# Output products of two attention layers as planned pieces, and bias tables by two rounded-format products

## The chip, the cores and the metric

The kernel runs on one core of one Trainium2 chip. The metric is the device time of one execution in microseconds (us). The engines are PE (TensorE, matrix products; PEld is its weight load), DVE (VectorE), ACT (ScalarE), POOL (GpSimd) and SP (SyncE, which here only issues transfers).

## The reference

All inputs are float32, one sequence of 256 tokens, model width 1024. Three blocks follow each other and share the residual `h`:

- Layer A: `h += dsa_mixer(rms_norm(h)) `, attention with 16 heads of 64. An indexer picks the best 64 keys per query; the logits get a bias `rel_bias[bucket(key - query)]` per head, then softmax, the product with `v`, and `out @ a_w_o` (1024 x 1024). An MLP with a squared ReLU follows (1024 to 4096 to 1024).
- Layer B: `h += mla_mixer(...)`, attention with 16 heads of 96 on low-rank keys and queries, and `out @ b_w_o` (1024 x 1024). The same kind of MLP follows.
- A hybrid layer: an mLSTM, three groups of dilated window attention with 8 heads each, whose logits get a bias from `rel_bias_2`, gates, an output product, and a gated MLP.

The changed parts are the two products `out @ a_w_o` and `out @ b_w_o` and the four bias tables: one of 16 heads for layer A, three of 8 heads for the window groups. A table holds, for each head, the bias at each of 512 relative positions. It is made as a product of the 32 bucket values (plus one row for positions that are masked) with a constant 0/1 matrix `c_oh` of 33 x 512.

## The kernel before

The 256 tokens are two tiles of 128, called t (0 and 1). Each large product is computed in a rounded float32 format (fp32r): an operand is split into a high part and a low rest (`split`, `wsplit`: the high part by a copy on ACT, the rest by a subtraction on DVE), and three products are summed: high x high, high x low, low x high (`mm_tok`, L275, L276, L278).

A weight piece is 512 contraction rows by 512 columns. It comes by one transfer of 1 MB on SP's queue (L247) into one of 3 `raw` buffers, and is split into one of 4 pairs of `hi`/`lo` buffers (L252 on ACT, L255 on DVE).

An output product of an attention layer is four PSUM banks, (t, ci) with ci the half of the 1024 columns. Each bank sums over two groups g of four contraction tiles, that is heads 0 to 7 and heads 8 to 15. A bank takes 24 products of 512 columns, 12 for each g. `out_proj` (L300) loads and splits the four weight pieces and then calls `mm_tok` for the four banks, t outermost. `add_res` (L315) adds a bank to the residual. The banks are the two buffers of the tag `acc`.

The order of instructions on each engine is made by a scheduler of the language from the program's order: an instruction that comes earlier in the program has the higher rank, and where it isn't ready, a later one may go first. Inside the attention layers the program's order is itself written out by hand. `weave` (L525) walks a plan: a name runs an item, `*n` runs n rounds of the attention pipeline, `**` all that are left. A round runs f1 of a step (logits, maximum, exponential), f2 of the step before (transposes of the probabilities) and f3 of the one before that (product with `v`). A step handles two heads of one token tile. In PLAN_A `s`, `k`, `q`, `t` are scores, top-k, query projection and its transposes. In PLAN_B `k`, `q`, `2`, `3` with a group number are key and query projections of four heads, their scaling, and their transposes into `KTb`/`QT`; `o` with t and a half is the transposes of the attention's output. `out_proj` stands behind the whole plan in both layers, so its instructions have the lowest rank there. Its weight splits are held behind chosen instructions (`behind`): in layer A behind the two top-k masks (`picked`), in layer B behind the last copies of the groups 2 and 3 (`made`).

A bias table is made by `bias_rows` (L438): the constant matrix comes by SP's queue into a buffer of the tag `pT` (2 buffers, also used by the attention for its transposed probabilities), one plain float32 product writes PSUM, ACT copies it, and ACT's queue stores it to memory. It is called once in layer A, before the attention, and three times in the first MLP. `rb` (L450) holds the bucket values, 16 columns for layer A and 24 for the window groups.

Of the kernel before, what the change touches and what calls it, by code (L numbers as in the profile page):

```python
# [10 lines left out]
F32 = mybir.dt.float32  # L11
# [6 lines left out]
P = 128  # L18
# [6 lines left out]
NACC, NTR, NLG, NPO = 2, 2, 3, 1  # L25


PLAN_A = "s0 k0 q0 q1 t00 t01 s1 * t10 k1 *4 t11 **"
PLAN_B = "k0 q0 k2 20 q1 k1 30 21 *2 q2 31 * 22 k3 q3 *2 32 *4 23 *2 o00 33 *5 o10 *2 o01 o11"
PLAN_C = "ck mg ms cq q0 mw k0 mn v0 v1 ml B0 *2 q1 *3 B1 *3 o0 k1 *3 k2 * v2 * q2 B2 o1 *2 a0 *2 a1 * b1 * p0 p1 *4 b0 *3"  # L30


# [57 lines left out]
def block_kernel(ctx: ExitStack, tc: tile.TileContext, a, out: bass.AP):  # L90
# [24 lines left out]
    def tpt(s):  # L115
        return sp.tile([P, 512], F32, tag="pT", name=nm(s), bufs=NPT)
# [171 lines left out]
    def dense_by_tile(jobs, holds=(None, None)):  # L288
# [5 lines left out]
        for t in range(2):  # L294
            for pr, (x, KT, _, _, n, _, evac) in zip(parts, jobs):
                ps = acc("acc")
                mm_tok(ps[:, :n], x, t, pr, KT)
                evac(t, ps[:, :n])

    def out_proj(x, w, scale=None, holds=(None, None)):  # L300
        dense_by_tile([(x, 8, w, 512 * ci, 512, None, lambda t, ps, ci=ci: add_res(t, ci, ps, scale))
                       for ci in range(2)], holds)
# [78 lines left out]
    def mlp(i):  # L381
# [46 lines left out]
        for c in range(2, 8):  # L428
            step(c - 2)
            up(c)  # L430
            if i == 0 and 3 <= c <= 5:
                bias_rows(c - 2, 33, 8, 8 * c - 8, vec_b[c - 3])
        last([6, 7], r2)

    def len_u(u):
        return u[0][0].shape[1]

    def bias_rows(which, K, M, c0, vec):  # L438

        oh = tpt("oh")  # L440
        nc.sync.dma_start(oh[:33, :], a["c_oh"][:, which, :])
        ps = trp("bt")
        PE.matmul(ps[:M, :], rb[:K, c0:c0 + M], oh[:K, :], start=True, stop=True)
        sb = tj("bts")
        A.activation(sb[:M, :], ps[:M, :], AF.Copy)
        nc.scalar.dma_start(vec, sb[:M, :])

    vec_a = dr.tile([16, 512], F32, name="vec_a")
    vec_b = [dr.tile([8, 512], F32, name=f"vec_b{g}") for g in range(3)]
    rb = cp.tile([33, 40], F32, name="rb")  # L450
    gcols = {}

    def ldk(dst, src):
        tc.keep_in_program_order(nc.sync.dma_start(dst, src))

    def load_consts():
        V.memset(rb[32:33, :], 1.0)
        chmask = t2("chmask")[:, :256]
        ldk(chmask, a["c_sq"][:, 512:768])
        ldk(rb[:32, 0:16], a["rel_bias"])  # L460
        ldk(rb[:32, 16:40], a["rel_bias_2"])
        for nm_, src in (("kv", a["kv_norm"]), ("q", a["b_attn_norm"][0])):
            gcols[nm_] = cp.tile([P, 8], F32, name="gc" + nm_)
            ldk(gcols[nm_], src.rearrange("(k p) -> p k", p=P))
        return chmask
# [108 lines left out]
    def layer_a():  # L574
# [24 lines left out]
                mm_tok(ps[:, :356], x, t, wkv[ci], 8)  # L599
                A.activation(kvi[t][:, ci * 356:(ci + 1) * 356], ps[:, :356], AF.Copy, scale=rs[t])  # L600
        chmask = load_consts()
        bias_rows(0, 32, 16, 0, vec_a)

        KT = t4("KT").rearrange("p (a n) -> p a n", a=4)
        qiT, w8 = [], []
# [71 lines left out]
        def q_T(t, ci):  # L677
            tp = transposes(qn[t, ci], 4)
            A.activation(qT[t][:, ci * 512:(ci + 1) * 512], tp, AF.Copy)
# [22 lines left out]
        for i in range(2):  # L702
            items["s%d" % i] = lambda i=i: scores(i)
            items["k%d" % i] = lambda i=i: topk(i)
            items["q%d" % i] = lambda i=i: dense(x, 8, w, [(512 * i, 512)], lambda t, _, ps: ev_q(t, i, ps), gain=gcol)
            for ci in range(2):
                items["t%d%d" % (i, ci)] = lambda i=i, ci=ci: q_T(i, ci)
        weave(PLAN_A, items, steps)
        out_proj(oT, a["a_w_o"][0], holds=picked)

    identb = cp.tile([P, P], BF, name="identb")
    V.tensor_copy(identb, ident)
# [1 line left out]
    def layer_b():  # L714
# [185 lines left out]
        for gi in range(4):  # L900
            for c, f in zip("kq23", proj(gi)):
                items[c + str(gi)] = f
        for c in '00 01 10 11 20 21 30 31'.split():
            steps += attend(int(c[0]), int(c[1]))
        for t in range(2):
            for i in range(2):
                items["o%d%d" % (t, i)] = lambda t=t, i=i: o_T(t, i)
        weave(PLAN_B, items, steps)
        out_proj(oT, a["b_w_o"][0], holds=(made[2], made[3]))

    def block2():
        w = a["w_in_2"][0]
# [413 lines left out]
```

## Time and profile before

| | |
|---|---|
| three runs, us | 1152.83, 1156.35, 1156.69; median 1156.35 |
| profiled execution | 1153.44 us, its span 1151.3 us |
| PE | 1124.7 us busy (98%), 6912 matrix products and transposes |
| PEld | 992.4 us (86%) |
| DVE, ACT, POOL | 678.6 us (59%), 614.1 us (53%), 68.4 us (6%) |
| granted clock of PE, mean | 0.998 |
| moved | 191.92 MB, 167 GB/s |

The span is counted from the profile's start; all stretches below are in us from there. A busy share is the time in which an engine had an instruction under way. Layer A's attention is worked on from about 56 to 114 us, the first MLP from 122 to 308, layer B's attention from about 340 to 398. In the rows, "idle before" stands in square brackets with what ended it.

### The profile page before, as it was taken

The numbers are of one execution on the slowest core, as the hardware profiler recorded it, in microseconds if no ns is written. First come the engines' busy times: TensorE is split into PE (matmuls) and PEld (weight loads), VectorE is DVE, ScalarE is ACT, GpSimd is POOL, SyncE is SP. The second block draws the span as 40 slices with busy tenths as digits, with TensorE's granted clock in tenths as the row PEclk, the third lists the DMA queues.
The fourth block names the chain that finished last, engine by engine and source line by source line (L and its number), as shares of the span: only waits on it lengthen the run. The fifth ranks groups of instructions, "written<-read, shape, count | busy, mean of one in ns | idle before, by whom it ended". The sixth has DMA issues, their size and how long they took to land.

```text
span 1151.3 us, 17271 instructions
## 1 busy us (share of the span) xinstructions
PE 1124.7 (98%) x6912; PEld 992.4 (86%) x6912; DVE 678.6 (59%) x1224; ACT 614.1 (53%) x1070; POOL 68.4 (6%) x80
## 2 busy tenths in 40 slices
PE   7989999999998999999999999999999999999997
PEld 6767898889897879989989999888888878999996
DVE  6794754445688574554366976645475566544544
ACT  7654555445487555554446664555554435433443
POOL 1210000000043000000000000010000030000000
PEclk9999999999999999999999999999999999999999
DMA  9540646554462346565538444744544535546641
GB/s 282 199 147 23 216 151 222 182 184 132 132 212 75 104 147 214 170 219 184 171 107 281 147 147 148 240 143 147 183 147 153 183 122 178 206 154 213 202 141 61
DMA packets 105383, 191.92 MB, mean 167 GB/s; under 512 B 6616, under 2 KB 22960, under 8 KB 105304
## 3 DMA queue, kind: packets, MB, share of 16 engines
q1 hardware_dynamic: 104056, 187.16, 48.6%
q0 software_dynamic: 1040, 3.54, 1.0%
q8 instruction: 54, 0.88, 0.3%
q14 instruction: 25, 0.20, 0.1%
q10 hardware_dynamic: 208, 0.13, 0.0%
HBM read 189.68 MB, written 1.13 MB: 166 GB/s over the span
## 4 chain that ended last, share of the span: by engine, by line
PE 92%; DVE 4%; ACT 1%; issue 1%; DMA 0%; POOL 0%; SPq 0%; POOLq 0%; DVEq 0%; ACTq 0%
PE acc L275 10%; PE acc L276 10%; PE acc L278 9%; PE dn L361 7%; PE dn L362 7%; PE dn L364 7%; PE up L310 5%; PE up L313 5%; PE up L311 5%; PE tr L165 3%; PE po L509 2%; PE qk L310 2%; PE qk L311 2%; PE lg L485 2%; PE qk L313 2%; PE fp L310 1%
## 5 line engine op out<-in xcount | busy, mean ns | idle before, releaser
L255 DVE TENSOR_TENSOR wlo<-raw,whi 128x1024 fp32r<-128x1024 f32 (+3 forms) x340 | 385.5, 1177 | 211.3 <-ACT whi L252 211.1
L252 ACT ACTIVATE whi<-raw 128x1024 fp32r<-128x1024 f32 (+3 forms) x340 | 322.9, 1007 | 212.3 <-PE dn L364 86.7
L310 PE MATMUL up<-mxh,whi 128*128 128x256 f32 x448 | 110.9, 281 | 0.0
L311 PE MATMUL up<-mxl,whi 128*128 128x256 f32 x448 | 110.7, 280 | 0.0
L361 PE MATMUL dn<-whi,uh 128*128 128x512 f32 x256 | 100.7, 395 | 0.0
L362 PE MATMUL dn<-wlo,uh 128*128 128x512 f32 x256 | 100.6, 394 | 0.0
L158 POOL TENSOR_TENSOR rr<-rv,mhalf 128x1 f32<-128x1 f32 (+2 forms) x42 | 39.8, 950 | 821.5 <-DVE rv L156 806.2
L310 PEld LDWEIGHTS up<-mxh,whi 128*128 128x128 f32 x448 | 84.3, 188 | 0.7
L311 PEld LDWEIGHTS up<-mxl,whi 128*128 128x128 f32 x448 | 84.2, 188 | 0.7
L275 PE MATMUL acc<-whi,cxh 128*128 128x512 f32 (+1 forms) x192 | 74.5, 389 | 0.0
L276 PE MATMUL acc<-wlo,cxh 128*128 128x512 f32 (+1 forms) x192 | 72.3, 378 | 0.0
L313 PE MATMUL up<-mxh,wlo 128*128 128x256 f32 x448 | 71.0, 280 | 0.0
L364 PE MATMUL dn<-whi,ul 128*128 128x512 f32 x256 | 69.5, 394 | 0.0
L313 PEld LDWEIGHTS up<-mxh,wlo 128*128 128x128 f32 x448 | 60.3, 188 | 0.0
L361 PEld LDWEIGHTS dn<-whi,uh 128*128 128x128 f32 x256 | 48.1, 188 | 13.2 <-ACT whi L252 2.6
L364 PEld LDWEIGHTS dn<-whi,ul 128*128 128x128 f32 x256 | 48.1, 188 | 11.2
L362 PEld LDWEIGHTS dn<-wlo,uh 128*128 128x128 f32 x256 | 48.1, 188 | 10.6
L278 PE MATMUL acc<-whi,cxl 128*128 128x512 f32 (+1 forms) x192 | 50.6, 382 | 0.0
L169 DVE TENSOR_TENSOR ul<-sq,uh 128x512 fp32r<-128x512 f32 x28 | 19.4, 692 | 51.8 <-ACT uh L169 51.5
L310 PE MATMUL qk<-cxh,whi 128*128 128x256 f32 x192 | 49.1, 287 | 0.0
L311 PE MATMUL qk<-cxl,whi 128*128 128x256 f32 x192 | 48.2, 282 | 0.0
L493 ACT ACTIVATE lg<-lg,nx 128x128 f32<-128x128 f32 (+1 forms) x80 | 35.4, 446 | 16.3 <-DVE nx L553 16.3
(414 smaller groups left out, 2410.2 us busy)
## 6 DMA issues: line engine op xcount, KB each, us to landing
raw<-in_w_in SPq DMA_DIRECT2D x38, 1024.0 KB, 5.2
raw<-in_mlp_w_up SPq DMA_DIRECT2D x32, 1024.0 KB, 5.3
raw<-in_mlp_w_down SPq DMA_DIRECT2D x32, 1024.0 KB, 5.1
raw<-in_w_gate SPq DMA_DIRECT2D x10, 1024.0 KB, 5.5
raw<-in_w_up SPq DMA_DIRECT2D x10, 1024.0 KB, 5.1
raw<-in_w_down SPq DMA_DIRECT2D x10, 1024.0 KB, 5.0
raw<-in_w_in SPq DMA_DIRECT2D x6, 688.0 KB
raw<-in_a_w_in SPq DMA_DIRECT2D x4, 1024.0 KB
```

The costliest lines, as they stand in the source:

```text
L158: G.tensor_tensor(r[:, :n], v[:, :n], mhalf[:, :n], op=OP.pow)
L252: A.activation(hi[:, c], raw[:, c], AF.Copy)
L255: V.tensor_tensor(lo[:, c], raw[:, c], hi[:, c].bitcast(F32), op=OP.subtract)
L275: PE.matmul(o, s0, wh[:, k, :], start=(g + k == 0), stop=False)
L276: PE.matmul(o, s0, wl[:, k, :], start=False, stop=False)
L278: PE.matmul(o, xs(xl, g + k, t), wh[:, k, :], start=False, stop=(g + k == KT - 1))
L310: PE.matmul(o, s0, xh[(g + k) // 4][:, (g + k) % 4, :], start=(g + k == 0), stop=False)
L311: PE.matmul(o, s0, xl[(g + k) // 4][:, (g + k) % 4, :], start=False, stop=False)
L313: PE.matmul(o, wl[:, k, col:col + P], xh[(g + k) // 4][:, (g + k) % 4, :], start=False, stop=(g + k == KT - 1))
L361: PE.matmul(ps, s0, wh[:, k, :], start=(c == 0 and k == 0), stop=False)
L362: PE.matmul(ps, s0, wl[:, k, :], start=False, stop=False)
L364: PE.matmul(ps, xs(u[1], k, t), wh[:, k, :], start=False, stop=(c == nc_ - 1 and k == kt - 1))
```

## The change

Three things are changed.

1. `out_proj` is no longer called for the layers A and B. `out_parts` adds items to the plan: `w0` and `w1` load and split the weight pieces of one half of the columns each, `m` with t, ci and g runs the 12 products of one bank and one g. A bank is taken at g = 0 and added to the residual after g = 1. The plans place these items among the last attention rounds. The holds of the splits stay the same.
2. In layer B the order of the attention's groups and tiles is changed (group 3's first tile comes before group 2's second), `23` comes one round earlier, `33` two, `o00` and `o10` two and four.
3. The bias tables are made by two fp32r products, of the high part and of the rest of `rb`. The two parts are tiles of 33 x 128, zeroed at the start by DVE and filled by four small copies on ACT and four subtractions on DVE. The constant matrix is converted to fp32r on its way in, and this transfer is issued by POOL. All 128 PSUM rows are written; the rows of table g begin at 32 g.

```diff
-PLAN_A = "s0 k0 q0 q1 t00 t01 s1 * t10 k1 *4 t11 **"
-PLAN_B = "k0 q0 k2 20 q1 k1 30 21 *2 q2 31 * 22 k3 q3 *2 32 *4 23 *2 o00 33 *5 o10 *2 o01 o11"
+PLAN_A = "s0 k0 q0 q1 t00 t01 s1 * t10 k1 *4 t11 w0 w1 *6 m000 * m001 * m010 * m011 * m100 * m110 ** m101 m111"
+PLAN_B = "k0 q0 k2 20 q1 k1 30 21 *2 q2 31 * 22 k3 q3 *2 32 *3 23 * o00 33 w0 w1 *2 o10 *3 o01 m000 * m001 * m010 * m011 * m100 m110 o11 m101 m111"
...
+    def out_parts(items, x, w, holds):
+        parts, banks = {}, {}
+        def load(ci):
+            with behind(holds(ci)):
+                parts[ci] = wparts(w, 8, 512 * ci, 512)
+        def run(t, ci, gi):
+            if gi == 0:
+                banks[t, ci] = acc("acc")
+            g, kk, (wh, wl) = parts[ci][gi]
+            ps = banks[t, ci]
+            for k in range(kk):
+                s0 = xs(x[0], g + k, t)
+                PE.matmul(ps, s0, wh[:, k, :], start=(g + k == 0), stop=False)
+                PE.matmul(ps, s0, wl[:, k, :], start=False, stop=False)
+            for k in range(kk):
+                PE.matmul(ps, xs(x[1], g + k, t), wh[:, k, :], start=False, stop=(g + k == 7))
+            if gi == 1:
+                add_res(t, ci, ps)
+        for ci in range(2):
+            items["w%d" % ci] = lambda ci=ci: load(ci)
+            for t in range(2):
+                for gi in range(2):
+                    items["m%d%d%d" % (t, ci, gi)] = lambda t=t, ci=ci, gi=gi: run(t, ci, gi)
...
-                bias_rows(c - 2, 33, 8, 8 * c - 8, vec_b[c - 3])
+                bias_rows(c - 2, 8, vec_b[c - 3])
...
-    def bias_rows(which, K, M, c0, vec):
-        oh = tpt("oh")
-        nc.sync.dma_start(oh[:33, :], a["c_oh"][:, which, :])
+    def bias_rows(which, M, vec):
+        oh = sp.tile([P, 512], F32R, tag="pT", name=nm("oh"), bufs=NPT)
+        G.dma_start(oh[:33, :], a["c_oh"][:, which, :])
         ps = trp("bt")
-        PE.matmul(ps[:M, :], rb[:K, c0:c0 + M], oh[:K, :], start=True, stop=True)
+        for i, r in enumerate(rbs):
+            PE.matmul(ps, r[:33, :], oh[:33, :], start=i == 0, stop=i == 1)
         sb = tj("bts")
-        A.activation(sb[:M, :], ps[:M, :], AF.Copy)
-        nc.scalar.dma_start(vec, sb[:M, :])
+        m = slice(32 * which, 32 * which + M)
+        A.activation(sb[m, :], ps[m, :], AF.Copy)
+        nc.scalar.dma_start(vec, sb[m, :])
...
+    rbs = [cp.tile([33, 128], F32R, name="rb" + e) for e in "hl"]
+    for r in rbs:
+        V.tensor_scalar(r, ident[:33, :], 0.0, None, op0=OP.mult)
...
-        V.memset(rb[32:33, :], 1.0)
+        V.memset(rb[32:33, 0:16], 0.0)
+        V.memset(rb[32:33, 16:40], 1.0)
...
-        bias_rows(0, 32, 16, 0, vec_a)
+        for g, (c0, n) in enumerate(((0, 16), (16, 8), (24, 8), (32, 8))):
+            A.activation(rbs[0][:33, 32 * g:32 * g + n], rb[:33, c0:c0 + n], AF.Copy)
+            V.tensor_tensor(rbs[1][:33, 32 * g:32 * g + n], rb[:33, c0:c0 + n], rbs[0][:33, 32 * g:32 * g + n].bitcast(F32), op=OP.subtract)
+        bias_rows(0, 16, vec_a)
...
+        out_parts(items, oT, a["a_w_o"][0], lambda ci: picked[ci])
         weave(PLAN_A, items, steps)
-        out_proj(oT, a["a_w_o"][0], holds=picked)
...
-        for c in '00 01 10 11 20 21 30 31'.split():
+        for c in '00 01 10 11 20 30 21 31'.split():
...
+        out_parts(items, oT, a["b_w_o"][0], lambda ci: made[2 + ci])
         weave(PLAN_B, items, steps)
-        out_proj(oT, a["b_w_o"][0], holds=(made[2], made[3]))
```

## Rows read from the trace of the kernel before

**Rows 1.** The page's busy times: us, share of the span, instructions.

```profile
PE 1124.7 (98%) x6912; PEld 992.4 (86%) x6912; DVE 678.6 (59%) x1224; ACT 614.1 (53%) x1070; POOL 68.4 (6%) x80
```

**Rows 2.** Busy time by stretch: length, then busy us (instructions) by engine, PE clock.

```profile
core 0: us, PE busy (x) PEld busy (x) DVE busy (x) ACT busy (x) POOL busy (x), PEclk, DMA share, GB/s
...
58.00:75.00 17.00, 13.39 (x76) 9.12 (x75) 16.72 (x68) 11.64 (x42) 3.42 (x3) 1.00 0.43 155
75.00:100.00 25.00, 24.93 (x137) 18.67 (x135) 18.21 (x55) 11.69 (x40) 0.00 (x0) 1.00 0.25 85
...
398.00:417.00 19.00, 18.58 (x84) 14.60 (x84) 10.55 (x16) 7.91 (x14) 0.57 (x1) 1.00 0.26 88
```

**Rows 3.** Bias product: group of its line, then PE's timeline around the first MLP's first.

```profile
L443 PE MATMUL bt<-oh,rb 33*8 33x512 f32 (+1 forms) x8 | 4.1, 591 | 0.0
...
191.72 1.02 PE L443 MATMUL bt<-oh,rb 33*8 33x512 f32 x2
192.67 0.50 PE L361 MATMUL dn<-whi,uh 128*128 128x512 f32 x1
```

**Rows 4.** The chain that ended last: one run of eight output products, 104 to 114.

```profile
109.91 1.86 PE acc L278 x8
```

**Rows 5.** PE's timeline, end of layer A: start, us, instruction, idle before.

```profile
102.47 0.66 PE L165 MATMUL tr<-ident,o 128*128 128x128 f32 x4 [1.27 <-DVE ss L177]
...
114.28 0.66 PE L165 MATMUL tr<-ident,o 128*128 128x128 f32 x4 [0.79 <-DVE o L697]
...
115.62 0.50 PE L275 MATMUL acc<-whi,aoh 128*128 128x512 f32 x1 [0.25 <-ACT aoh L169]
...
122.17 0.47 PE L275 MATMUL acc<-whi,mxh 128*128 128x512 f32 x1 [0.31 <-DVE h L318]
```

**Rows 6.** PE's timeline, layer B's attention: its four waits from 360 to 398.

```profile
365.77 0.44 PE L165 MATMUL tr<-ident,p 128*128 128x128 f32 x2 [0.82 <-DVE QT L850]
...
368.03 0.94 PE L509 MATMUL po<-kvb,pT 128*128 128x64 f32 x4 [0.71 <-DVE pT L502]
...
373.68 0.77 PE L165 MATMUL tr<-ident,p 128*128 128x128 f32 x2 [1.19 <-ACT p L493]
...
391.21 0.77 PE L165 MATMUL tr<-ident,p 128*128 128x128 f32 x2 [0.49 <-ACT p L493]
```

**Rows 7.** Busy time by stretch around those waits, columns as in rows 2.

```profile
368.00:370.00 2.00, 1.97 (x9) 1.93 (x10) 2.00 (x4) 1.39 (x6) 0.00 (x0) 0.56 0.01 4
370.00:372.00 2.00, 2.00 (x10) 1.68 (x8) 2.00 (x3) 0.00 (x0) 0.00 (x0) 0.58 0.78 213
```

**Rows 8.** ACT's timeline in layer B: the output weights' splits and what follows.

```profile
364.14 3.89 ACT L252 ACTIVATE whi<-raw 128x1024 fp32r<-128x1024 f32 x4
367.93 0.56 ACT L493 ACTIVATE p<-lg,nb,scq 128x256 f32<-128x256 f32 x1
...
382.03 3.89 ACT L252 ACTIVATE whi<-raw 128x1024 fp32r<-128x1024 f32 x4
```

**Rows 9.** Chain in layer B, 360 to 398: transposes of group 3's keys.

```profile
380.98 0.43 PE tr L165 x4
```

**Rows 10.** Timeline of the first 25 us, all engines.

```profile
8.04 0.16 DVE L177 TENSOR_TENSOR ss<-ss 128x1 f32<-128x1 f32 x1 [3.92 <-ACT sq L175]
...
19.27 0.19 PEld L275 LDWEIGHTS acc<-whi,axh 128*128 128x128 f32 x1 [0.85 <-ACT whi L260]
...
21.69 0.73 ACT L260 ACTIVATE whi<-raw,gca 128x512 fp32r<-128x512 f32 x1 [1.23 <-DMA raw<-in_a_w_in]
...
24.16 0.24 ACT L615 ACTIVATE dup<-dup 128x64 f32<-128x64 f32 x1
```

**Rows 11.** Transfers: SP's own waits; POOL's timeline; issues with KB and us to landing.

```profile
SPq L441 <- DVE pT L502: 26.3, 1, 26.3
...
64.82 0.63 POOL L138 DMA_DIRECT2D gain<-in_mlp_norm  x1
...
gain<-in_mlp_norm POOLq DMA_DIRECT2D x2, 512.0 KB, 3.9
```

## Prediction, made before the changed kernel was run

> **What bounds the kernel now.** I read the page's busy times first: PE has an instruction under way for 1124.7 of 1151.3 us, DVE and ACT for little more than half [rows 1]. So time can come from two places only: PE work that disappears, and the 26.6 us in which PE stands. The table by stretch shows where it stands in the layers that are changed: 17.00 - 13.39 = 3.6 us from 58 to 75, almost nothing (0.07) from 75 to 100 [rows 2]. Then PE's timeline gives the single waits: in layer A's end 1.27, 0.79, 0.25 and 0.31 us, together 2.62 [rows 5]; in layer B's attention 0.82, 0.71, 1.19 and 0.49 us, together 3.21 [rows 6]. The reader should see that each of these is short, and that PE waits for DVE or ACT, never for a transfer. Last, the granted clock: from 368 to 372, right behind two of layer B's waits, it is 0.56 and 0.58 [rows 7], near the lower of the two levels (1.2 of 2.4 GHz) for most of 4 us. At the full clock that work would have taken 2.00 x 0.56 + 2.00 x 0.58 = 2.28 us, so this costs 1.72 us more. What layer B's attention loses is thus 3.21 + 1.72 = 4.93 us.
>
> A run of eight output products lasts 1.86 us in the chain, 0.233 us each [rows 4]. The two output products have 96 each, 22.4 us per layer. The change moves them; it does not remove one.
>
> **Part 1, the three tables in the first MLP.** PE starts one at 191.72 and the next product at 192.67: 0.95 us for a table [rows 3]. The stretch has no waits, so this is all on the path. Two fp32r products of 512 columns at 0.233 make 0.47. If so, 0.48 x 3 = 1.45 us are saved. Bounds: 0, if a product with 33 rows streams no faster in the new format (two records of 0.475 as now), and 1.45. No row has fp32r with 33 rows, but every fp32r product of 512 columns in the trace is at 0.233; I take 1.45. The transposing, the ACT copy and the store stay.
>
> **Part 2, layer A's table and the two new tiles.** This table's product is nearly free today: at 19.27 PE's weight load has stood 0.85 us for `whi`, and the 0.95 us product lies over that wait [rows 10]. In the new kernel it needs four copies on ACT and four subtractions on DVE first. A small copy on ACT is 0.24 us, a small operation on DVE 0.16 [rows 10]: 0.96 and 0.64 us. Behind them on ACT stand the splits of layer A's weights, for which PE waits. Their cover is ACT's wait of 1.23 us for a weight at 21.69 [rows 10]; if the copies fall there they cost nothing, if they fall ahead of it they cost up to 0.96, and the product, no longer under a wait, 0.47. DVE's two zero fills need only the identity, and DVE stands 3.92 us up to 8.04 [rows 10], so I cost them at nothing (0.32 without that cover). Bounds 0 to 1.75, taken: +0.4, for the product itself.
>
> **The moved transfers.** Four loads of 66 KB go from SP to POOL. On SP the first two of the MLP's stood 26.3 us for a `pT` buffer [rows 11], with weight loads behind them; those weights needed buffers of their own that came free later, since PE at the MLP's start waits for the residual and not for weights [rows 5]. So their going frees nothing, and I cost it at nothing. On POOL an issue is 0.63 us, and even 512 KB land in 3.9 [rows 11]; the tables are needed tens of us later, and layer A's has the time from the start to about 19 [rows 10]. What is behind them on POOL are reciprocal roots, of which the first MLP has one near its start and none until its end. So nothing again; without that cover it is 3.9 us once.
>
> The POOL row above was taken in a stretch in which DVE was busy 16.72 of 17.00 us [rows 2], and it still took 0.63. The Trainium skill, "SBUF — State Buffer", in its box on how DVE blocks DMA, speaks against this move: descriptors of a POOL transfer wait while DVE runs in a mode that holds the port shared with POOL, and it gives some 620 ns growing to 3100. By the page's figure the issue would be 2.5 us longer, an estimate, and the sum as much higher if PE stood for it; the row shows no such growth.
>
> **Part 3, layer A's pieces.** From 75 to 100 PE is full [rows 2]: the scheduler already fills the attention's holes with single products from `out_proj`, although they rank last. So only the end can gain, 2.62 us. Its largest wait, 1.27 at 102.47, arises because token tile 0's products are used up and its residual additions stand on DVE in front of the attention's output. With higher rank, tile 0's pieces end earlier, and those additions no longer fall there; half of that wait, 0.6 to 0.7, is what I count. The other three belong to the last chain (output, transposes, split, products), which has the same length. Taken: -0.7. Bounds: -2.62, and +2.0, if pieces go ahead of attention rounds and the end lacks cover: about the waits of 1.27 and 0.79 once more.
>
> **Part 4, layer B's pieces and order.** The 19 us from 398 to 417 are dense, 18.58 busy [rows 2]: a store of independent products that stands behind the attention. The waits of 3.21 us lie before it. But pieces can't fill the waits at 365 to 374, since the first output transposes (`o00`) only come after the last of these waits. What can fill them is `33`, two rounds earlier: 16 transposes, four at 0.43 [rows 9], 1.72 us, and the logits of group 3 behind them. And tile 0's second half is ready two steps earlier, which covers the 0.49 at 391. Against it stands the source of these waits: ACT splits four weight parts in one go, 3.89 us from 364.14, and the exponentials that the transposes wait for begin at 367.93 [rows 8]. The holds are the same, so this clump stays, and the second one (at 382.03, today covered by products) comes nearer. I take 40% of 4.93: -2.0. Bounds: -4.93, and +5.6, if the second clump is uncovered as well: 3.89 us and 1.72 us of low clock behind it.
>
> **Sum.** -1.45 + 0.4 - 0.7 - 2.0 = -3.75 us. Against the profiled execution's own 1153.44 (1151.3 of span and 2.1 around it) that is 1149.7. The median of the runs, 1156.35, is 2.9 us above the profiled one; my forecast is for a median, so 1156.35 - 3.75 = **1152.6 us**.
>
> **Rivals.** I call 0.5% of the time, 5.8 us, about what a measurement of this kernel can tell from no change.
>
> *All waits close.* The new order in layer B takes away the waits from 365 to 374 and with them the dip of the clock, which is there only behind waits. For it: every wait is under 1.3 us and there are 18.58 us of independent work near [rows 2]. Against it: the clump on ACT. It gives -1.45 + 0.4 - 1.3 - 4.9 = -7.25, with all of layer A's -9: 1147 to 1149, faster.
>
> *Nothing is gained by moving.* PE was filled by low-rank products already; what is left of the waits is chain length. Only the tables count: -1.45 + 0.4 = -1.05, 1155.3, the same.
>
> *The splits come ahead of the attention.* Place: ACT and DVE in layer B, where `w0` and `w1` now rank above the last nine rounds. If `w1`'s clump falls before `o00` is split, PE has nothing to run while the exponentials wait: +5.6, less the tables' 1.05, is +4.6, 1160.9; with layer A's +2.0 also, 1162.9, slower by over 0.5%. It decides from the point at which a clump lies more than about 1 us inside a stretch without output products to run; at 364 it did so already [rows 6, 8], at 382 not.
>
> *POOL's loads come late.* By the rule of the port above, PE would stand at a table until its matrix lands, up to 3.9 us [rows 11] once: -3.75 + 3.9, 1156.5, the same. By the Trainium skill's page "SBUF — State Buffer" (the box named above) this is what a move to POOL invites; the trace has one POOL issue under a busy DVE, without it.
>
> **How the numbers follow.** Chances: my forecast 0.43, all waits close 0.25, nothing gained by moving 0.18, splits ahead 0.09, late loads 0.05. All of "all waits close" is faster; of "splits ahead" most reaches the bound, as its price is rough; the rest is the same. Faster 0.25, same 0.66, slower 0.09. The forecast's own range is 1149.5 to 1155.5. For 8 in 10 I go down into "all waits close" (1147 less half a us) and up to where "splits ahead" begins to count: **1146.5 to 1159.5**. The runs themselves differ by 3.9 us, which lies within.
>
> **What the profile afterwards would show.** Part 1: a table's two products 0.23 to 0.25 us apart, and 0.5 us from the first one's start to the next product in the first MLP. Part 2: ACT's small copies in its wait at 21, PE not later at the first weights. Part 3: the wait before the output's transposes at 102 below 0.7, with the same start of the first MLP or up to 1 us earlier. Part 4: waits in layer B's attention of 1 to 2 us in place of 3.2, a clock of 1.00 there, and the MLP behind it some 3 us earlier in all. The prediction is wrong if the table products are not shorter, if a new wait of over 1 us for ACT's exponentials stands between 370 and 385, or if PE stands at a table for its matrix.

## The result, and the profile after

The changed kernel takes 1162.98 us (median of 7 runs, 1162.04 to 1166.23) against 1156.35 for the kernel before on the same chip (7 runs, 1152.83 to 1159.63): ratio 1.0073, 95% interval 1.0057 to 1.0090. (The ratios here and below are those on record, worked out from all runs of both kernels; they are not quotients of the two medians, which give 1.0057 here.) The forecast was 1152.6 with a range to 1159.5; the time lies above the range, on the other side of "no change".

The profiled execution took 1165.82 us (span 1163.9 and 1.9 around it), 12.38 us over that of before. Its busy times on the page:

```profile
PE 1131.2 (97%) x6912; PEld 1000.1 (86%) x6912; DVE 679.0 (58%) x1231; ACT 615.7 (53%) x1074; POOL 70.7 (6%) x84
```

PE has the same 6912 instructions as before [rows 1], but is busy 6.5 us longer and idle 6.1 us longer (32.7 of the span, 26.6 before). The same instructions taking longer points to a lower clock: its mean is 0.992 in this execution, 0.998 in that of before. Where the time goes, the first events of each part on PE's timeline tell. Each stretch in us:

| stretch on PE's timeline | before | after | difference |
|---|---|---|---|
| start to first MLP's first product | 122.17 | 125.38 | +3.21 |
| first MLP, to layer B's first product | 186.23 | 185.35 | -0.88 |
| layer B up to its first output product | 70.46 | 68.80 | -1.66 |
| from there to the second MLP's first product | 37.97 | 48.09 | +10.12 |
| the rest, with what lies around the span | 736.61 | 738.20 | +1.59 |

The first and the fourth stretch lose 13.3 us together. The third, shorter by 1.66, is not a gain: PE runs 16 instructions fewer in it and 16 more in the fourth, so work has moved across the border between the two, and PE stands 4.27 us in it (68.80 - 64.53), 3.41 before. The third and fourth stretch by engine, before and then after, columns as in [rows 2]:

```profile
308.40:378.86 70.46, 67.05 (x422) 61.43 (x423) 61.44 (x190) 57.38 (x144) 23.87 (x24) 0.98 0.45 144
378.86:416.83 37.97, 36.95 (x207) 30.28 (x206) 23.00 (x41) 18.90 (x40) 0.57 (x1) 1.00 0.30 98
...
310.73:379.53 68.80, 64.53 (x406) 59.10 (x407) 59.60 (x184) 55.44 (x135) 24.14 (x24) 0.98 0.46 147
379.53:427.62 48.09, 43.66 (x223) 35.87 (x221) 24.96 (x47) 22.30 (x48) 0.57 (x1) 0.89 0.18 58
```

PE's timeline of the changed kernel in both layers, with the idle time before an instruction and what ended it:

```profile
85.42 1.10 PE L519 MATMUL lg<-KT,qT 128*128 128x512 f32 x2 [1.60 <-DVE nx L587]
...
103.43 0.66 PE L165 MATMUL tr<-ident,o 128*128 128x128 f32 x4 [0.78 <-DVE o L734]
...
114.98 1.10 PE L543 MATMUL po<-kvi,pT 128*128 128x64 f32 x8 [1.36 <-ACT pT L534]
...
116.87 1.11 PE L165 MATMUL tr<-ident,o 128*128 128x128 f32 x4 [0.78 <-DVE o L734]
...
373.66 0.44 PE L165 MATMUL tr<-ident,oB 128*128 128x128 f32 x2 [0.75 <-ACT pT L534]
375.18 0.64 PE L165 MATMUL tr<-ident,k 128*96 128x128 f32 x4 [1.08 <-DVE pT L536]
...
393.20 0.92 PE L165 MATMUL tr<-ident,p 128*128 128x128 f32 x2 [1.88 <-ACT p L527]
...
421.15 0.50 PE L316 MATMUL acc<-whi,boh 128*128 128x512 f32 x1 [1.85 <-ACT boh L169]
...
427.62 0.50 PE L275 MATMUL acc<-whi,mxh 128*128 128x512 f32 x1 [0.62 <-DVE h L346]
```

These answer to [rows 5, 6]. The 1.27 before the transposes at 102 has shrunk to 0.78 (not by the pieces, as the part on the prediction shows), but 1.60, 1.36, 1.88 and 1.85 are new, and layer B's waits between 366 and 376 are still there: 0.81, 0.71, 0.33, 0.75 and 1.08, together 3.68. Busy time and PE's clock by stretch, columns as in [rows 2]:

```profile
116.00:118.00 2.00, 1.22 (x7) 1.13 (x7) 0.69 (x1) 0.00 (x0) 0.53 (x1) 0.70 0.04 11
118.00:120.00 2.00, 2.00 (x7) 1.57 (x7) 1.35 (x2) 1.19 (x2) 0.00 (x0) 0.50 0.08 23
120.00:122.00 2.00, 2.00 (x9) 1.57 (x9) 2.00 (x3) 0.00 (x0) 0.00 (x0) 0.95 0.00 0
...
376.00:384.00 8.00, 8.00 (x36) 7.00 (x35) 1.58 (x4) 5.67 (x9) 0.00 (x0) 0.57 0.37 127
392.00:400.00 8.00, 6.79 (x22) 5.49 (x23) 3.51 (x11) 4.44 (x17) 0.00 (x0) 0.58 0.43 161
```

Behind three groups of waits, those of 114 to 117, of 366 to 376 and the one at 393, the granted clock is near 0.50, the lower level of 1.2 GHz; behind the 1.60 at 85 and the 1.85 at 421 it is 1.00. From 376 to 384 PE's work takes 8.00 x 0.43 = 3.44 us longer by it, from 392 to 400 8.00 x 0.42 = 3.36, together 6.8 against 1.72 in the profiled run of before [rows 7]. The first of the two low stretches follows the group of waits that the kernel before has too.

Who is late? ACT's timeline at the end of layer A before the change (first two lines), then at both ends of the attention after it:

```profile
110.00 0.60 ACT L500 ACTIVATE pT<-tr 128x512 f32<-128x512 f32 x1 [5.75 <-PE tr L165]
110.88 3.90 ACT L252 ACTIVATE whi<-raw 128x1024 fp32r<-128x1024 f32 x4 [0.28 <-PE acc L278]
...
110.55 3.90 ACT L252 ACTIVATE whi<-raw 128x1024 fp32r<-128x1024 f32 x4 [5.33 <-PE acc L319]
114.36 0.58 ACT L534 ACTIVATE pT<-tr 128x512 f32<-128x512 f32 x1
...
418.61 2.00 ACT L252 ACTIVATE whi<-raw 128x1024 fp32r<-128x1024 f32 x2 [0.75 <-PE acc L319]
420.52 0.58 ACT L169 ACTIVATE boh<-tr 128x512 fp32r<-128x512 f32 x1
```

The four `whi` are the next MLP's first weights. Each bracket says that an output product (`acc`, L319) ended ACT's wait: the last products of a weight part give its buffer back, the MLP's weight takes it, and ACT, in order, splits it in front of the copy for which the attention's last step waits. Before, the same splits ran at 110.88, but behind the last `pT` copy of the attention. The early pieces change the order: eight output products that ran behind the last transposes of the probabilities now run ahead of them. So these transposes come at 112.18 in place of 109.30 (1.9 us of that is the pieces', by e2 below, the rest the tables'), and the first four of the products release the splits before them. I call such a run of splits a clump. DVE's half of these splits is held behind the last `put`; ACT's half is not.

The tables, PE's timeline in the first MLP, for [rows 3]:

```profile
194.89 0.50 PE L472 MATMUL bt<-oh,rbh 33*128 33x512 f32 x1
195.23 0.39 PE L472 MATMUL bt<-oh,rbl 33*128 33x512 f32 x1
195.55 0.51 PE L389 MATMUL dn<-whi,uh 128*128 128x512 f32 x1
```

From the table's start to the next product it is 0.66 us, 0.95 before.

### The profile page after: what moved, and what is told of

Same layout as the page of the kernel before. It is cut to its first block, busy times and chain, and to the rows that moved or that the text cites. A ratio compares the mean times of both kernels' runs of the same rounds, so it can differ in the third digit from the quotient of the medians.

```text
span 1163.9 us, 17282 instructions
## 1 busy us (share of the span) xinstructions
PE 1131.2 (97%) x6912; PEld 1000.1 (86%) x6912; DVE 679.0 (58%) x1231; ACT 615.7 (53%) x1074; POOL 70.7 (6%) x84
## 4 chain that ended last, share of the span: by engine, by line
PE 90%; DVE 5%; ACT 2%; issue 1%; DMA 1%; POOL 1%; SPq 0%; POOLq 0%; DVEq 0%
PE acc L275 8%; PE acc L278 8%; PE acc L276 8%; PE dn L389 7%; PE dn L390 7%; PE dn L392 7%; PE up L338 5%; PE up L339 5%; PE up L341 5%; PE tr L165 4%; PE po L543 2%; PE lg L519 2%; PE qk L339 2%; PE qk L338 2%; PE qk L341 2%; DVE wlo L255 2%
```

## The experiments

All were timed in five rounds beside the kernel before, whose median was 1155.9 to 1157.0 in these sessions, with runs from 1152.6 to 1161.1. "A", "B att." and "B end" are stretches of each profiled run on PE's timeline: from layer A's first output product to the first MLP's first product, from layer B's first product to its first output product, from there to the second MLP's first product. Each is of one execution, the profiled one; the median is of all.

| run | median us | ratio, 95% interval | A | B att. | B end |
|---|---|---|---|---|---|
| before | 1156.35 | 1 | 46.47 | 70.46 | 37.97 |
| after | 1162.98 | 1.0073 [1.0057, 1.0090] | 49.69 | 68.80 | 48.09 |
| e1_tables | 1158.74 | 1.0014 [0.9996, 1.0031] | 47.39 | 70.10 | 37.96 |
| e2_a_pieces | 1160.39 | 1.0034 [1.0019, 1.0049] | 48.89 | 74.10 | 38.65 |
| e3_b_all | 1161.14 | 1.0045 [1.0030, 1.0059] | 46.44 | 69.36 | 45.46 |
| e4_b_order | 1156.63 | 1.0002 [0.9989, 1.0015] | 46.47 | 69.48 | 42.68 |
| e5_hold | 1160.15 | 1.0032 [1.0016, 1.0048] | 47.98 | 69.46 | 44.02 |
| e6_a_rank | 1153.95 | 0.9992 [0.9975, 1.0010] | 46.48 | 70.04 | 37.96 |
| e7_b_rank | 1157.00 | 1.0006 [0.9991, 1.0021] | 46.47 | 69.35 | 41.84 |
| e8_b_w | 1161.39 | 1.0039 [1.0025, 1.0054] | 46.46 | 69.34 | 44.49 |
| e9_a_hold | 1156.62 | 0.9994 [0.9979, 1.0009] | 46.99 | 72.50 | 38.56 |
| e10_b_w1 | 1155.77 | 0.9985 [0.9974, 0.9996] | 46.48 | 69.38 | 41.03 |
| e11_all_rank | 1156.40 | 0.9994 [0.9982, 1.0005] | 47.47 | 69.57 | 42.80 |
| e12_tab_a | 1158.63 | 1.0012 [0.9998, 1.0026] | 47.45 | 74.36 | 38.46 |
| e13_b_w0 | 1152.25 | 0.9967 [0.9952, 0.9981] | 46.45 | 64.01 | 43.22 |
| e14_w0 | 1150.99 | 0.9956 [0.9941, 0.9970] | 46.46 | 66.54 | 38.67 |
| e15_best | 1152.59 | 0.9971 [0.9956, 0.9986] | 47.37 | 63.99 | 41.85 |
| e16_w0_tab | 1151.52 | 0.9962 [0.9948, 0.9977] | 47.41 | 66.74 | 38.69 |
| e17_w0_a | 1150.80 | 0.9958 [0.9944, 0.9972] | 46.45 | 66.75 | 38.69 |

**One part at a time.** The theory after the traces: the rank of the product pieces costs the time, in each layer by itself; rivals were the order, the early weights and the tables.

*e1_tables*: of the change, only the tables (PLAN_A, PLAN_B, the order and `out_proj` as before).

> The tables alone (the two fp32r products, POOL's loads), layers A and B as before. Theory (ranked pieces cost the time): the first MLP is about 0.9 us shorter and nothing else changes, so 0.5 to 1.5 us under the kernel before, ratio 0.998 to 1.000. Rival (the tables shift layer A's schedule on ACT and DVE, and the 3.2 us of layer A come from that): the first MLP starts some 3 us later than at 122.2, and the whole is 1 to 3 us over the kernel before.

*e2_a_pieces*: only layer A's pieces. *e3_b_all*: only layer B's pieces and order. *e4_b_order*: layer B's order and plan, with `w` and `m` taken out of it and `out_proj` behind:

```diff
-PLAN_B = "... *2 32 *4 23 *2 o00 33 *5 o10 *2 o01 o11"
+PLAN_B = "... *2 32 *3 23 * o00 33 *2 o10 *3 o01 * * * * o11"
-        for c in '00 01 10 11 20 21 30 31'.split():
+        for c in '00 01 10 11 20 30 21 31'.split():
```

> Layer A's pieces alone, tables and layer B as before. Theory (pieces ranked ahead of the last rounds leave the last chain without cover): the first MLP starts 2 to 4 us later than at 122.2, with a new wait of over 1 us before the last product with v; ratio 1.002 to 1.004. Rival (the tables did it): start at 122 to 123, ratio within 0.001 of 1.

> Layer B's pieces and order alone, tables and layer A as before. Theory: this is where most of the loss lies: from the first output product to the second MLP 44 to 48 us in place of 37.9, less 1.7 us gained ahead of it; in all 4 to 8 us over the kernel before, ratio 1.004 to 1.007. Rival (layer B's loss comes from where the clock's low stretches happen to fall after a shifted layer A): 0 to 2 us over.

> Layer B's new order of groups and items alone, with the output product behind the plan as before; tables and layer A as before. Theory (the pieces' rank costs the time, the order gains): the 1.7 us gained ahead of the first output product stay, the second MLP starts 0 to 3 us earlier than at 416.8, ratio 0.997 to 1.000. Rival (the order is the cause: the second clump of splits comes earlier, at 380 to 384 with the first tile of group 3 behind it, and the exponentials wait): 4 to 8 us over the kernel before, as with the pieces.

The pieces cost 0.34% in layer A, and 0.45% in layer B with the order; the order alone and the tables cost nothing that the intervals can tell from no change. 1160.39 - 1156.15 and 1161.14 - 1156.15 are 4.2 and 5.0 us: together 9.2, more than the 6.6 of the whole. The table says why they don't add: in e2's profiled run A is only 2.4 us longer, and "B att.", whose code is untouched, 3.6 us; the whole change has no such 74.10 there. (In the new order `o10` comes five rounds earlier, where the section on the change says four.)

**Rank or clump?** *e5_hold* is the whole change with ACT's half of the MLPs' first splits held too:

```diff
 def mlp(i):
-        holds = [tuple(mark[1:])]
+        holds = [tuple(mark)]
```

> The whole change, and ACT's halves of the splits of both MLPs' first weights (up_tok(0)) held behind ACT's copy of the attention's last output part, as DVE's halves are already. Theory of the clump (ACT splits the MLP's first weights in front of the attention's last pT and boh copies, 3.90 us at 110.55 and 2.00 us at 418.61): the waits of 1.36 at 114.98 and 1.85 at 421.15 fall below 0.9, the clock behind 116 stays at 1.00, first MLP's first product near 123 in place of 125.4; time 3 to 5 us below the changed kernel, 1158 to 1160, ratio to the kernel before 1.001 to 1.004. Rival (the cover is gone because tile 1's products ran ahead; the clump only fills a hole that is there anyway): the same time or worse, since the weights now come later than the residual, 1162 to 1166, ratio 1.005 to 1.009, first MLP's first product at 125 or later.

It gave 1160.15, a ratio of 1.0032 against the changed kernel's 1.0073; the 1.36 and the 1.85 are gone (at 422.02 a wait of 1.07 for the residual is left), and the first MLP starts at 123.18. So the clump costs time, but not all of it.

*e6_a_rank* takes layer A's pieces alone and lets token tile 1 rank behind the attention; *e7_b_rank* does so with all of layer B's pieces; *e8_b_w* leaves the pieces early and ranks the weights later:

```diff
-PLAN_A = "... m000 * m001 * m010 * m011 * m100 * m110 ** m101 m111"
+PLAN_A = "... m000 * m001 * m010 * m011 ** m100 m110 m101 m111"
-PLAN_B = "... w0 w1 *2 o10 *3 o01 m000 * m001 * m010 * m011 * m100 m110 o11 m101 m111"
+PLAN_B = "... w0 w1 *2 o10 *3 o01 *4 o11 m000 m010 m001 m011 m100 m110 m101 m111"
+PLAN_B = "... *2 o10 *3 o01 w0 w1 m000 * m001 * m010 * m011 * m100 m110 o11 m101 m111"
```

> Layer A's pieces alone, on the kernel before, but token tile 1's four pieces all rank behind the last attention round (loads w0, w1 and tile 0's pieces stay early). Theory of the rank (m100 and m110 run ahead of the last transposes and leave the end without cover): first MLP's first product back at 122 to 123 in place of 125.9, no low clock at 118 to 122, time 1155 to 1157.5, ratio 0.999 to 1.001. Rival (the early rank of the weight splits, or of tile 0's pieces, costs): as with all of layer A's pieces, 1159 to 1161, ratio 1.003.

> Layer B's order and weights as changed, on the kernel before, but all eight product pieces rank behind the last output transpose (w0, w1 stay early, behind 33). Theory of the rank (tile 0's pieces ahead of the last rounds uncover the end): stretch from the first output product to the second MLP's first product back to 38 to 41 us (48.1 in the changed kernel, 37.9 before), time 1156 to 1158, ratio 0.999 to 1.002. Rival (the early weights: their splits on ACT come ahead of the exponentials at 385 to 392 and take the clock down): the wait of 1.4 to 1.9 before the transposes near 393 and the low clock behind it stay, 1159 to 1162, ratio 1.003 to 1.005.

> Layer B's pieces and order as changed, on the kernel before, but the weights w0 and w1 rank behind o01 and so behind three more attention rounds. Theory of the rank of the pieces: the end stays uncovered, waits of 1 to 2 us near 420 stay, 1159.5 to 1162, ratio 1.003 to 1.005. Rival (the clump of w1's splits ahead of the exponentials is the larger part): the wait near 393 and the low clock at 394 to 400 go, 3 us less than with all of layer B's part, 1157 to 1158.5, ratio 1.001 to 1.002.

By their medians e6 and e7 are back at the kernel before; e8 is not. The rank of the pieces decides, not that of the weights. In layer A, e6 has PE's order of before again. e8 shows too that a load's rank doesn't say when its splits run: w1's `whi` still ran at 380.12, as soon as its hold let it. *e9_a_hold* is e2 with the hold of e5 in the first MLP alone:

> Layer A's pieces alone on the kernel before (4 us slower by themselves), with ACT's halves of the first MLP's first splits held behind ACT's copy of the last output part. The theory that ACT's clump does most of the damage in layer A: ratio 1.000 to 1.0015, 1156.5 to 1158.5, the wait before the last values product 0.3 us or less in place of 1.36, clock 1.00 from 114 to 124, first product of the MLP at 123 to 123.5. The theory that the missing cover does it, the clump only filling a hole: 1.0025 to 1.004, 1159.5 to 1161, and the wait stays above 1 us with another releaser.

0.9994: the hold alone gives back what layer A's pieces cost, with tile 1's products as early as before. ACT's timeline of this run against that above, the copies now first and the clump behind them:

```profile
112.56 0.60 ACT L528 ACTIVATE pT<-tr 128x512 f32<-128x512 f32 x1 [7.65 <-PE tr L165]
115.80 0.60 ACT L169 ACTIVATE aoh<-tr 128x512 fp32r<-128x512 f32 x1 [2.63 <-PE tr L165]
116.29 3.90 ACT L252 ACTIVATE whi<-raw 128x1024 fp32r<-128x1024 f32 x4
```

So in layer A the early rank does its harm by way of the clump. What is left, 0.5 us (46.99 against 46.47), is not missing cover either: the last values products start 35.9 us after the first output product in both kernels. Most of it is the clump in its new place, in front of the copy of `mxh` (0.31 before, [rows 5]):

```profile
123.35 0.47 PE L275 MATMUL acc<-whi,mxh 128*128 128x512 f32 x1 [0.65 <-ACT mxh L169]
```

In layer B the hold is not enough: e5's end is 44.02 long, e7's 41.84. e5 has the wait of 1.07 at 422 and a clock of 0.55 and 0.59 from 392 to 396, e7 0.18 and 1.00 there.

**Layer B's wait near 392.** It is in the order alone too (1.40 before the transposes at 390 to 392 in e4, e7 and e8). DVE's timeline of e7 shows whose it is:

```profile
384.28 4.62 DVE L255 TENSOR_TENSOR wlo<-raw,whi 128x1024 fp32r<-128x1024 f32 x4
388.82 0.41 DVE L530 COPY pT<-tr 128x256 f32<-128x256 f32 x1
389.15 1.34 DVE L896 TENSOR_REDUCE mx<-lg 128x2 f32<-128x256 f32 x3
```

w1's four subtractions stand in front of the maxima of group 3's logits, and ACT's exponentials wait for those. In the changed kernel it is the same: the subtractions from 385.68 on, the maxima at 390.55. *e10_b_w1* holds w1 behind `o10`'s put instead:

```diff
-PLAN_B = "... o00 33 w0 w1 *2 o10 *3 o01 *4 o11 m000 ..."
+PLAN_B = "... o00 33 w0 *2 o10 w1 *3 o01 *4 o11 m000 ..."
-        out_parts(items, oT, a["b_w_o"][0], lambda ci: made[2 + ci])
+        out_parts(items, oT, a["b_w_o"][0], lambda ci: made[2] if ci == 0 else tuple(mark))
```

> Layer B's order, all product pieces behind the last transpose, and the second weight w1 ranked behind o10 and its splits held behind o10's put, so that DVE's four subtractions (4.62 us at 384.28) no longer stand in front of the maxima of group 3. Theory of the DVE clump: the wait of 1.40 before the transposes near 392 falls below 0.7 and the low clock behind it goes; stretch from the first output product to the second MLP's first product 38 to 40 us in place of 41.8; 1153.5 to 1156, ratio 0.997 to 0.9995. Rival (the wait is the length of the chain of group 3, or w1 then comes too late for the products that fill the attention): the same or a longer stretch, 1156 to 1160, ratio 0.9995 to 1.003.

The maxima now begin at 383.86, that wait is 0.50, and the clock behind it is 1.00: 0.9985. The stretch, 41.03, is longer than forecast: PE waits 0.54 at 391 for w1's `wlo`, and low clock from 372 to 380 is still there, most of it ahead of the stretch.

*e11_all_rank* is the whole change with the plans of e6 and e7:

> The whole change with both ranks mended: layer A's token tile 1 and all of layer B's pieces rank behind the attention, the tables and layer B's order stay. Theory of the rank: what the pieces cost goes, 1155 to 1157.5, ratio 0.998 to 1.001. Rival (the costs of the parts do not add, something else in the sum costs): 1158.5 to 1161, ratio 1.002 to 1.004.

0.9994: by the medians, everything that the change costs goes with the rank. The new order is not free for all that. "B att." and "B end" are together 112.37 us in e11, 111.19 in e7 and 112.16 in e4, against 108.43 before, and no run of these three has a mean clock above 0.997; the kernel before reaches 0.998 in many of its runs and 0.994 in others, and its median lies between.

*e12_tab_a* is e6 with the tables. I expected 1152.5 to 1154.5 if both small gains are real, 1156 to 1158.5 if the tables only shift which runs keep the full clock. It gave 1158.63.

**The earlier clump, and the runs' spread.** The waits from 366 to 376 remain, in every kernel so far. e2, e9 and e12 have layer B's code of before, yet their "B att." is 74.10, 72.50 and 74.36: the low clock after those waits lasted 12, 8 and 12 us there, 4 us in the profiled run of before and not at all in e1's and e6's (70.10 and 70.04). Where the low clock lies decides what it costs. In the profiled run of before it lies ahead of the wait for the exponentials, 1.19 at 373.68 [rows 6]; in e6, without low clock, the same wait is longer by 0.88:

```profile
374.11 0.77 PE L165 MATMUL tr<-ident,p 128*128 128x128 f32 x2 [2.07 <-ACT p L521]
```

So those 4 us cost 0.4 us (70.46 against 70.04 and 70.10), not 1.72. In e2, e9 and e12 the low clock comes behind that wait, and their "B att." is 2.4 to 4.3 us longer than that of e1 and e6. The runs of the kernel before fall roughly into groups by their mean clock: near 1153.6 us at 0.998, near 1156.5 at 0.995, near 1158.8 at 0.994. With the tables and this layer B, 9 of e1's 12 runs and 10 of e12's lie above 1157.5 us, against 10 of 32 and 15 of 34 of the kernel before beside them: the tables raise the share of long runs, by a way that no run here shows.

*e13_b_w0* is e10 with w0's splits held too, behind `o00`'s put; *e14_w0* is the kernel before with that hold alone; *e15_best* is e13 with the tables. The edit of e14 (e13 and e15 hold both weights by `lambda ci: tuple(mark)` in `out_parts`):

```diff
         def o_T(t, i):
             ...
             put(oT, i, t, tp)
+            made[t, i] = tuple(mark)
-        out_proj(oT, a["b_w_o"][0], holds=(made[2], made[3]))
+        out_proj(oT, a["b_w_o"][0], holds=(made[0, 0], made[3]))
```

> As the run with w1 behind o10's put, and w0's splits too held, behind o00's put, so that ACT's clump of 3.89 us at 364.73 leaves the place in front of the exponentials at 368.52. Theory (that clump makes the waits of 0.6 to 0.8 from 366 to 374, and these the low clock from 372 to 379): waits there below 1.5 us in sum in place of 3.3, clock 1.00 from 366 to 380, 1151 to 1153.5, ratio 0.995 to 0.9975. Rival (w0 then comes late: the first output products stand for it near 378): the same 1155 to 1157 with a new wait for whi, ratio 0.998 to 1.000.

> The kernel before with one hold changed: w0's splits in layer B behind o00's put. Theory: the waits at 365.77, 368.03 and 373.68 (2.72 us) shrink to 1.5 or less, no low clock behind them in any run, so the time is at the lower end of the kernel before's or below: 1151 to 1153.5, ratio 0.995 to 0.998, and the runs lie within 2 us of each other. Rival (the waits are the length of the chain, or w0 comes late): 1155 to 1158, ratio 0.999 to 1.001, runs 5 us apart as now.

> The tables and the layer B of the run with both weights held, layer A as before. If the theory of the dip holds and the tables' 0.85 us comes through: 1150 to 1152.5, ratio 0.994 to 0.9965, 0.5 to 1.5 us below the run without the tables. If the tables give no time: as that run.

e14 takes 1150.99 us, and all its runs lie between 1150.0 and 1152.0. PE's timeline and the stretches of e14, to be set against [rows 6, 7]:

```profile
366.75 0.44 PE L165 MATMUL tr<-ident,p 128*128 128x128 f32 x2 [0.62 <-DVE QT L850]
...
377.31 0.50 PE L276 MATMUL acc<-wlo,boh 128*128 128x512 f32 x1 [0.69 <-DVE wlo L255]
...
389.20 0.77 PE L165 MATMUL tr<-ident,p 128*128 128x128 f32 x2 [0.50 <-ACT p L493]
```

```profile
366.00:370.00 4.00, 3.38 (x28) 3.15 (x27) 3.51 (x12) 2.12 (x10) 0.00 (x0) 1.00 0.42 131
370.00:374.00 4.00, 4.00 (x36) 3.84 (x35) 2.82 (x8) 3.34 (x14) 0.00 (x0) 1.00 0.00 0
374.00:378.00 4.00, 3.23 (x23) 2.60 (x22) 3.29 (x6) 4.00 (x6) 0.00 (x0) 1.00 0.02 4
```

The waits at 368 and 374 are gone, the clock stays at 1.00. The price of the later weight is one wait of 0.69 for `wlo` at 377. e13, which has the new order and both holds, is slower than e14 in the same session (1152.25 against 1150.99; "B att." and "B end" together 107.23 against 105.21): once w0's clump is gone, the new order, with w1's hold, costs time. e15, with the tables, is no faster than e13.

**The tables without the noise.** *e16_w0_tab* and *e17_w0_a* add to e14 the tables, or layer A's pieces as in e6.

> The kernel before with w0's splits in layer B behind o00's put (1150.99 us, runs from 1150.0 to 1152.0), and the tables in the new format. If the 0.85 us of the first MLP come through: 1149.8 to 1150.5, ratio 0.9945 to 0.9955. If something in the later stages takes them back, as the run with the new order suggests: 1150.8 to 1151.8, ratio 0.9955 to 0.9965.

> The same hold, and layer A's pieces with token tile 1 behind the attention, tables as before. If the forecast of -0.7 for the attention's waits in layer A was right apart from the rank: 1150.0 to 1150.6. If nothing is to be had there: 1150.7 to 1151.5.

Neither moves the time by more than the runs differ; both came out by their second branch. For the tables the profile says where the 0.81 us of the first MLP (185.38 against 186.19 in e14) go. First, layer A: A is 47.41 against 46.46, 0.95 longer, as in all kernels with the tables. e16 is still ahead of e14 by 0.47 us at the last third (first product of `yah`, 875.41 against 875.88), since its A begins 0.82 earlier, at 76.13 against 76.95. But that start lies anywhere from 75.5 to 77.2 in the kernels without the tables, so it can't be put down to them. From the second MLP on, the two run alike until ACT's last instruction. Then this one ends at 1145.42 and the span at 1150.0, 4.58 later; in e14 it is 1145.88 and 1149.3, 3.42 later. The transfers of e16 from 1144 to its end, by queue:

```profile
q1 hardware_dynamic: 288, 0.52, 23.8%
q14 instruction: 1, 0.01, 0.3%
```

The q14 line, a load of instructions, stands behind ACT's last instruction in the four kernels that have the tables and not the change's own pieces in both layers (e1, e12, e15, e16), and each of them ends 4.5 to 4.6 us after ACT's last instruction. None of the others has it there; they take 3.35 to 3.7 us (the changed kernel 3.64). That the load causes the 1.1 us is argued from this coincidence, not shown.

## Why the prediction was wrong

**Part 1** had the sign and mis-sized the term: -0.88 us where -1.45 stood. Two products of 0.34 and 0.32 take a table's place, not of 0.233. Nor is every such product at 0.233, as the prediction had it: the MLP's next one behind a table took 0.34 before as well (from 192.67 to 193.01, [rows 3]). The forecast read the rate of a long run off [rows 4]; a table is a run of two. Why these take longer is not shown.

**Part 2** came out near by luck. The tables alone put the first MLP 0.1 us later (122.28 against 122.17), +0.4 forecast. On ACT it went as thought: the four copies take 0.51 us at 20.54, ahead of a wait of 0.93 that was 1.23. But the sum priced PE and ACT only. The new work also shifts layer A's DVE order: with the tables, a wait of 1.60 appears near 85 and the 1.27 near 102 is 0.78. A is 47.4 in the runs with the tables and none of token tile 1's early pieces, 46.5 in those without either: +0.9, a term that the sum did not have. In e1 an earlier start of A by 0.8 hides it; the starts differ by more than that without the tables.

**The moved transfers** were right at nothing: POOL's four issues take 0.53 to 0.56 us, and no product waits for a table. The rival "POOL's loads come late", from the rule in the Trainium skill, "SBUF — State Buffer", box on how DVE blocks DMA, did not come true: no issue grew toward the figures given on that page. But this case hardly tests the rule. None of the issues fell beside a DVE copy: DVE stood during the issues at 2.50 and 113.92, and ran an attention output's product and a weight's subtractions during those at 116.63 and 195.91; at the forecast's own row, 64.82, it ran no copy either.

**Part 3 is the step that failed first**: "with higher rank, tile 0's pieces end earlier". They did not. In e2, which has layer A's pieces alone, PE runs the attention in the order and at the times of before, counted from the first output product, up to the eight products named above. The residual addition in front of the wait starts 24.69 us after the first output product in both, and the wait is 1.27 in both. The prediction's own remark, that the scheduler already fills the holes with these products although they rank last, holds for them too. The 0.78 in the changed kernel, which looks like the shorter wait that I counted on (it is 0.49 less), is in every kernel with the tables, e1 too, and in none without: luck. And e17 found no -0.7 to be had. What the rank did move are the eight products ahead of the last transposes, which I kept as a mere bound of +2.0. Measured: +3.2 us up to the first MLP in the profiled run, of which 0.9 are the tables', and +2.4 in A with layer A's part alone. The means, not named in the prediction, is the buffer that the early products give back and the MLP's splits on ACT that follow.

**Part 4 failed too**, in the step "what can fill them is `33`, two rounds earlier". It did not fill the waits from 365 to 374: they are 3.68 us in the changed kernel, 2.72 before (3.64 in e6). -2.0 was forecast, -1.66 + 10.12 = +8.5 measured in the profiled run, and the -1.66 is moved work. What came instead lay beyond the bound of +5.6: the 1.88 for w1's subtractions (named by the rival "the splits come ahead of the attention", but for ACT and for another place), the 1.85 at 421 (not named), and low clock worth 6.8 us from 376 to 400 where I had priced one dip of 1.72. Of the 6.8, 3.44 follow the old group of waits and lie partly ahead of the first output product at 379.53; 3.36 follow the 1.88. None of the prediction's three signs of being wrong shows this: the tables' products are shorter, PE stands at no table, and the new wait for exponentials stands at 393, not between 370 and 385.

**The rival** "the splits come ahead of the attention" gave 1160.9 to 1162.9 and had a chance of 0.09: nearest to the time, with the right kind of mechanism. That its sum comes so near is partly luck, as its 3.89 on ACT and its one dip of 1.72 are not the terms that were measured. Its own condition, a clump more than 1 us inside a stretch without output products, was met at 385 on DVE, at 110 and at 418 on ACT. I weighed it by [rows 8], where the second clump was covered, and did not ask what the early pieces would take from that cover.

**The 4.93** that layer B's attention was said to lose was misread as well. The 1.72 of low clock in it cost 0.4, since a wait behind it shrank. In other runs the low clock lasts up to 12 us behind that wait, which no single profile shows. e14 got 4.9 us by the medians with one hold, without any piece being moved: 3.2 of it against the profiled run of before (105.21 for "B att." and "B end" against 108.43), the rest from the low clock of other runs.

The +1.30 us of the changed kernel between 600 and 880 remain open: PE has no new wait there and its clock is 1.00; e3, e5 and e8 have them too, e4, e7, e10 and e11 not, so they go with layer B's early pieces.

## What to carry to other kernels

Before ranking independent work above a chain's last rounds, ask what its end releases: here a buffer that came free ahead of the chain's last copy started the next stage's splits, and ACT ran those in front of it. A load's rank did not delay its conversion (e8); a hold on an instruction of the same engine did, and a hold on one of two engines was half a hold. Before a shorter wait is put down to the change that was meant to shorten it, look for it in the runs that have only the other parts. Low clock that lay ahead of another wait cost little (0.4 us of 1.7). When a cluster of short waits comes before low clock, remove the clump that makes the cluster first: here that was worth 0.44%, and it narrowed the runs' spread from 6 to 2 us, in which smaller gains can be seen at all.

## What the hardware showed that I had not expected

Behind a cluster of waits of 0.2 to 2.3 us each, PE's clock was granted near 0.50 for 3 to 12 us, in which PE was nearly always busy; identical code got anything from none to 12 us of it (B att. 70.04 to 74.36). Ahead of a wait, 4 us of it cost 0.4. And a kernel's end is not fixed: 3.35 to 3.7 us from ACT's last instruction to the end of the span in fifteen profiled kernels, 4.5 to 4.6 in four, those with an instruction load behind ACT's last instruction.
